# An encoder on one core: TensorE's products too in a computed order, the last down group in other pieces, the final norm's squares through banks

## The chip, the core and the metric

The kernel runs on one core of a Trainium2 chip. The metric is device time in microseconds (us), as the median of several executions. One execution is also recorded by the hardware profiler; the profile's own clock runs from the first to the last instruction of the program (the span). Engines are named as in the profile: PE is TensorE (matrix products; PEld are its weight loads, which overlap the products), DVE is VectorE, ACT is ScalarE, POOL is GpSimd, SP is SyncE, which here only issues transfers (DMAs). SBUF is the on-chip memory that all engines use; a bank is one of eight pieces of the memory into which TensorE writes its sums.

## The reference

Two layers of an encoder over 512 tokens of width 1024, everything in float32. Each layer adds three things to x, and a last norm ends it:

```python
for l in range(DEPTH):
    x = x + hybrid_mixer(rms_norm(x, norm_mix[l]), w_in[l], na_rpb[l], gqa_q_norm[l], gqa_k_norm[l], w_out[l], rows, cos, sin)
    x = x + memory_cross_attention(rms_norm(x, norm_mem_q[l]), rms_norm(mem, norm_mem_kv[l]), w_mem_q[l], w_mem_kv[l], w_mem_o[l])
    x = x + conv_ffn(rms_norm(x, norm_ffn[l]), w_up[l], conv_w[l], conv_b[l], w_down[l])
return rms_norm(x, norm_final)

def conv_ffn(h, w_up, conv_w, conv_b, w_down):
    u = h @ w_up                                   # 1024 -> 2 x 2816
    up = jnp.pad(u, ((0, 0), (1, 1), (0, 0)))
    u = up[:, :-2] * conv_w[0] + up[:, 1:-1] * conv_w[1] + up[:, 2:] * conv_w[2] + conv_b
    gate, val = jnp.split(u, 2, axis=-1)
    return (jax.nn.silu(gate) * val) @ w_down      # 2816 -> 1024

def rms_norm(x, g):
    return x * lax.rsqrt(jnp.mean(x * x, axis=-1, keepdims=True) + EPS) * g
```

The mixer holds neighbourhood attention (8 heads) and grouped-query attention (8 heads over 2 key heads, with normed and rotated queries and keys) on one projection of x; the memory attention has 4 heads over 256 memory tokens.

## The kernel before

**Data.** x is kept transposed: eight tiles xT[0..7], each 128 features x 512 tokens. A float32 product is made of three fast ones: each operand is split into a rounded part hi and a rest lo, and `mm3` (L730) adds hi x hi, hi x lo and lo x hi in one bank. So every weight piece is loaded ("raw", two buffers), cast on ACT into hi (L647) and subtracted on POOL into lo (L648); hi and lo have four buffers each (`N_W`), and `get_w` (L651) emits the splits of the next two pieces (`AHEAD`) when one is taken.

**Stages.** In each layer: projections woven with the two attentions (`weave`, with `Filler` handing out projection products between the attention's steps), the memory attention, then the feed-forward part, with its 22 chunks of the inner width in three groups, `GROUPS = [(0, 8), (8, 7), (15, 7)]`. A chunk's up products (two of 24 products of 512 columns) are followed by the convolution and the gate on DVE and ACT (`up_finish`, L1617), whose result acts[j] is again a hi and lo pair. After a group's chunks its down products add to xT.

**The last group.** `down_last` (L1666) does layer 2's third group, chunks 15 to 21, and the final norm with it, in two halves of 256 tokens. For each of the eight rows m it sums 7 x 3 products of 256 columns in a bank; DVE adds the bank to xT[m] (L1704); `Norm.square` (L833) squares the row on ACT (L835) into an SBUF tile and DVE adds it to the running sum of squares (L843, L846), the last square staying apart; DVE scales the row by the norm's gain (`scale`, L1674). In the first half the first four rows leave out the last chunk at first (`N_LATE`). Weight pieces are 7 x 128 columns of one row m, loaded once for both halves: the first two pieces are in the hi and lo buffers, six in tiles of the "r" pool ("Pr" in `plan_down`), so that they are still there in the second half. `Norm.stat` (L849) sums over the features with small products against a column of ones, first for the running sum, then for the last square, each followed by warm-up products in the second half, and POOL makes the power -1/2 (L867). `Norm.spread` (L869) spreads it over a bank with products against the identity (L798), and ACT copies the bank to SBUF (L801). `finish` multiplies: DVE takes the bank for six rows (L1684), POOL the copy for two (L1682); five DMAs write the half's output. The first half's statistics and finish stand after rows 1 and 3 of the second half.

**What sets the order.** The program is emitted as a list per engine. PE and SP keep the written order: `PE` is a `Counted(InOrder)`, whose `keep` marks each product. For ACT, DVE and POOL the class `Order` (L306) computes an order at the end of the program (L1729). It models every instruction's duration (`Step.times`), the buffers and the transfers; `due` (L393) gives each instruction a latest start, counted back from the products, which are taken to follow one another; `run` (L411) plays the program, and `choose` picks on each free engine the ready instruction with the earliest latest start. Where a product comes more than 150 ns late in the model, its due time is moved forward by that (`credit`) for the next of 16 rounds; the round with the earliest end is kept. An engine on the chip executes its list strictly in that order.

Of the kernel before, what the change touches and what calls it, by code (L numbers as in the profile page):

```python
# [1 line left out]

# [16 lines left out]
P = 128  # L19
# [12 lines left out]
GROUPS = [(0, 8), (8, 7), (15, 7)]  # L32
EPS = 1e-6
# [19 lines left out]
N_RAW, N_W, N_R, N_T, N_S, AHEAD, AHEAD_HELD, N_WARM, N_LATE, N_FIRST = 2, 4, 21, 14, 24, 2, 5, 7, 4, (8, 16)  # L53
# [18 lines left out]
class Counted(InOrder):  # L72
# [4 lines left out]
    def matmul(self, out, lhsT, rhs, **k):  # L77
        n = 1
        for d in rhs.shape[1:]:
            n *= d  # L80
        self.ns += max(107.0, (n + 32) / 2.4)
        return self.keep(self.engine.matmul(out, lhsT, rhs, **k))  # L82


class Free:


    def __init__(self, engine):
        self.engine = engine

    def __getattr__(self, name):
        return getattr(self.engine, name)
# [110 lines left out]
ROUNDS = 16  # L203
# [102 lines left out]
class Order:  # L306

    FREE = ("ACT", "DVE", "POOL")  # L310

    def __init__(self, tc, kept):
# [98 lines left out]
    def run(self):  # L411
# [3 lines left out]
        ready, free_at = [0.0] * n, dict.fromkeys(HAND_OVER, 0.0)  # L415
# [9 lines left out]
        order, late, product = {e: [] for e in self.FREE}, [], None  # L425
# [3 lines left out]
        def earliest(j):  # L429
# [18 lines left out]
            return max(t, free_at[steps[j].engine])  # L448

        def choose(e):  # L450

            known = [(t, j) for j in open_[e] for t in [earliest(j)] if t is not None]
# [39 lines left out]
        def over_(s, t, end):  # L492

            for q in self.after[s.index]:
                need[q] -= 1
                begun = s.engine == "PE" == steps[q].engine or (s.index, q) in self.loose
                ready[q] = max(ready[q], t if begun else end + self.wait(s, steps[q]))
                if not need[q] and steps[q].engine in self.FREE:
# [7 lines left out]
        while len(issued) < n or moving:  # L506
            best = None
            for e in HAND_OVER:
                if e in self.FREE:
                    c = choose(e)  # L510
                elif at[e] < len(written[e]):
# [16 lines left out]
            if e in self.FREE:  # L528
                open_[e].remove(j)
                order[e].append(s)  # L530
            else:
                at[e] += 1
# [12 lines left out]
            free_at[e] = t + s.busy  # L545
            issued.add(j)
            for name in s.names:
# [5 lines left out]
            if s.dma:  # L553
                if not moving:
                    clock = max(clock, t)
                moving.append([t + DMA_NS, s.bytes, j])
            else:
                over_(s, t, t + s.takes)
# [5 lines left out]
def encoder_kernel(ctx: ExitStack, tc: tile.TileContext, t: dict, out: bass.AP):  # L564
    nc = tc.nc
    kept = set()
    PE, SP = Counted(tc, nc.tensor, kept), InOrder(tc, nc.sync, kept)
# [65 lines left out]
    def emit_split(act=ACT, cuts=2):  # L633
# [6 lines left out]
        if eng[1:] == "r":  # L640
            hi, lo = rtile((nk, ncol)), rtile((nk, ncol))
        else:
            hi = wpool.tile([P, nk, ncol], F32R, tag="hi", name=nm("hi"))
            lo = wpool.tile([P, nk, ncol], F32R, tag="lo", name=nm("lo"))
# [6 lines left out]
    def get_w(key, ahead=AHEAD):  # L651
# [3 lines left out]
        while ahead < min(len(plan), n + 1 + AHEAD_HELD) and plan[ahead][4][1:] == "r":  # L655
            ahead += 1
# [137 lines left out]
    def row_rep(rstd, n, tag, bufs, copy):  # L794

        pr = ps_t()
        for b in range(n):
            PE.matmul(pr[:, b * P : (b + 1) * P], rstd[:, b : b + 1].to_broadcast([P, P]), ident,  # L798
                      start=True, stop=True)
# [1013 lines left out]
```

## Time and profile before

| | us |
|---|---|
| median of 3 executions | 1351.61 (1350.64 to 1352.07) |
| the profiled execution | 1351.96 |
| its span | 1350.1 |
| PE busy | 1337.5 |
| DVE busy | 902.1 |
| POOL busy | 698.8 |
| ACT busy | 681.0 |

The granted clock of TensorE is 0.999 of full speed over the span. In the rows below, `L82` is the line of the helper through which every product goes, so products are told apart by their tiles: `mm<-r,hi` is a sum in an "mm" bank from a tile of the "r" pool and one of the hi buffers. A row of the timeline gives start, duration, engine, line, operation, tiles and shape; consecutive instructions of a kind are merged (x84), and brackets hold the engine's idle time before it and what ended it. A row of the chain gives start, length and what it consists of. A row of the stretches gives the stretch, its length, and then each engine's busy time and number of instructions, the granted clock, the DMA share and GB/s. Products are pipelined: the shown time of one overlaps the next.

### The profile page before, as it was taken

What the parts mean: (1) busy time and instruction counts of PE and PEld (TensorE: products, weight loads), DVE (VectorE), ACT (ScalarE), POOL (GpSimd) and SP (SyncE); (2) the same over time, 40 slices, a digit from 0 to 9 for tenths busy, and PEclk for the clock granted to TensorE, in tenths of its full rate; (3) what the DMA queues carried; (4) which work ended last, traced back from release to release, by engine and by line L of the source; (5) the groups of instructions that cost most, each with busy time, mean ns of one, the idle gap of its engine ahead of it and who ended that gap; (6) DMA issues with size and microseconds to landing.
All of it is one profiled execution on the core that took longest, in us unless ns stands there. A gap on an engine that the chain in (4) does not pass through costs nothing.

```text
span 1350.1 us, 19133 instructions
## 1 busy us (share of the span) xinstructions
PE 1337.5 (99%) x7018; PEld 1146.4 (85%) x7018; DVE 902.1 (67%) x1598; ACT 681.0 (50%) x1258; POOL 698.8 (52%) x483
## 2 busy tenths in 40 slices
PE   9999999999999999999999999999999999999997
PEld 7898899888888888888898888988888888888887
DVE  6678874775984388178546678746769825862874
ACT  6776676564442244233557667855644423432441
POOL 2558766626444443443744576655554444444541
PEclk9999999999999999999999999999999999999999
DMA  7773222313333333332455531233233333333321
GB/s 217 201 190 109 79 63 73 116 45 96 96 103 98 94 94 94 109 94 82 127 155 164 140 106 49 79 95 94 63 94 98 104 94 94 93 95 109 90 83 63
DMA packets 219214, 139.88 MB, mean 104 GB/s; under 512 B 6000, under 2 KB 212080, under 8 KB 219120
## 3 DMA queue, kind: packets, MB, share of 16 engines
q1 hardware_dynamic: 218432, 138.13, 35.4%
q8 instruction: 56, 0.92, 0.3%
q10 hardware_dynamic: 688, 0.52, 0.1%
q14 instruction: 38, 0.31, 0.1%
HBM read 126.05 MB, written 2.10 MB: 95 GB/s over the span
## 4 chain that ended last, share of the span: by engine, by line
PE 93%; DVE 2%; DMA 1%; issue 1%; ACT 1%; POOL 1%; SPq 0%; DVEq 0%; POOLq 0%; ACTq 0%
PE mm L82 81%; PE sc L82 7%; PE tr L69 4%; PE tr L82 1%; DMA raw<-in_w_down 1%; POOL r L648 1%; DMA xT<-in_xT 0%; DVE t L846 0%; DMA raw<-in_w_in 0%; ACT r L1075 0%; SPq L69 0%; DVE r L875 0%; ACT hi L647 0%; ACT t L1257 0%; DVE r L1684 0%
## 5 line engine op out<-in xcount | busy, mean ns | idle before, releaser
L648 POOL TENSOR_TENSOR lo<-raw,hi 128x1024 fp32r<-128x1024 f32 (+2 forms) x268 | 511.5, 1919 | 498.6 <-ACT hi L647 494.7
L82 PE MATMUL mm<-xg,hi 128*128 128x512 f32 x1920 | 595.0, 391 | 0.0
L82 PEld LDWEIGHTS mm<-xg,hi 128*128 128x128 f32 x1920 | 356.1, 188 | 70.9
L647 ACT CAST hi<-raw 128x512 fp32r<-128x512 f32 (+2 forms) x276 | 226.3, 839 | 318.8 <-PE mm L82 267.8
L82 PE MATMUL mm<-xg,lo 128*128 128x512 f32 x960 | 373.9, 389 | 0.0
L82 PE MATMUL mm<-r,hi 128*128 128x512 f32 (+1 forms) x1096 | 316.3, 372 | 0.6 <-DVE r L1641 0.5
L1635 DVE SCALAR_TENSOR_TENSOR t<-t,par,t 128x7 f32<-128x7 f32 (+1 forms) x352 | 251.2, 773 | 25.0 <-ACT t L1628 25.0
L82 PEld LDWEIGHTS mm<-r,hi 128*128 128x128 f32 x1096 | 198.6, 189 | 35.6 <-DVE r L1641 0.7
L82 PEld LDWEIGHTS mm<-xg,lo 128*128 128x128 f32 x960 | 180.2, 188 | 37.9
L82 PE MATMUL mm<-r,lo 128*128 128x512 f32 (+1 forms) x548 | 203.6, 372 | 0.0
L82 PEld LDWEIGHTS mm<-r,lo 128*128 128x128 f32 x548 | 103.3, 188 | 17.9
L881 POOL TENSOR_SCALAR t<-t,s 128x512 f32<-128x512 f32 (+1 forms) x112 | 67.9, 622 | 75.0 <-DVE s L1323 36.1
L1620 DVE TENSOR_TENSOR t<-mm,rep 128x512 f32<-128x512 f32 x88 | 60.0, 686 | 63.0 <-PE mm L82 47.3
L1664 DVE TENSOR_TENSOR xT<-xT,mm 128x512 f32<-128x512 f32 x32 | 22.0, 686 | 104.5 <-PE mm L82 104.5
L1640 ACT CAST r<-t 128x512 fp32r<-128x512 f32 x44 | 27.3, 620 | 101.7 <-DVE t L1638 101.7
L1638 DVE TENSOR_TENSOR t<-t,t 128x512 f32<-128x512 f32 x44 | 68.2, 1551 | 4.3 <-ACT t L1637 0.5
L82 PE MATMUL sc<-r,r 128*128 128x256 f32 (+1 forms) x352 | 70.7, 333 | 0.3 <-DVE r L1081 0.3
L1628 ACT ACTIVATE t<-t,par 128x512 f32<-128x512 f32 x88 | 67.0, 806 | 1.2 <-DVE t L1620 1.2
L1317 ACT ACTIVATE t<-sc,s,qr 128x512 f32<-128x512 f32 x64 | 49.3, 775 | 32.2 <-DVE s L881 32.2
L82 PE MATMUL mm<-r,r 128*128 128x256 f32 (+1 forms) x428 | 62.5, 297 | 1.7 <-POOL r L648 1.1
L69 PE MATMUL tr<-ident,t 128*128 128x128 f32 x456 | 61.0, 273 | 0.7 <-DVE s L1267 0.7
L82 PEld LDWEIGHTS mm<-r,r 128*128 128x128 f32 x428 | 56.4, 191 | 5.0 <-POOL r L648 1.3
(160 smaller groups left out, 1607.8 us busy)
## 6 DMA issues: line engine op xcount, KB each, us to landing
raw<-in_w_up SPq DMA_DIRECT2D x88, 512.0 KB, 3.8
raw<-in_w_in SPq DMA_DIRECT2D x33, 512.0 KB, 4.1
raw<-in_w_down SPq DMA_DIRECT2D x32, 448.0 KB, 3.7
raw<-in_w_mem_kv SPq DMA_DIRECT2D x16, 512.0 KB, 3.8
raw<-in_w_down SPq DMA_DIRECT2D x16, 512.0 KB, 4.0
r<-in_bias SPq DMA_DIRECT2D x16, 384.0 KB, 4.9
r<-r SPq DMA_DIRECT2D x22, 256.0 KB, 5.6
raw<-in_w_out SPq DMA_DIRECT2D x8, 512.0 KB, 3.7
```

The lines of the kernel that those rows point to most:

```text
L69: return lambda *a, **k: self.keep(op(*a, **k))
L82: return self.keep(self.engine.matmul(out, lhsT, rhs, **k))
L647: act.copy(hi[:, k], raw[:, k])
L648: (POOL if eng[0] == "P" else DVE).tensor_sub(lo[:, k], raw[:, k], f(hi)[:, k])
L881: eng.tensor_scalar(e, e, sums[:, col : col + 1], 1.0, op0=ALU.mult, op1=ALU.mult)
L1317: ACT.activation(e, sc[j], AF.Exp, bias=nmx[:, c], scale=qrs[i][:, col : col + 1], accum_out=sums[:, c])
L1620: DVE.tensor_mul(u, us[side], ffn.rep)
L1628: ACT.activation(cc, u, AF.Identity, bias=par[:, l, CB + ch : CB + ch + 1], scale=w[1])
L1635: DVE.scalar_tensor_tensor(cc[:, dst], u[:, src], wi, cc[:, dst], op0=ALU.mult, op1=ALU.add)
L1638: DVE.tensor_mul(cs[0], cs[0], cs[1])
L1640: ACT.copy(acts[j][0], cs[0])
L1664: DVE.tensor_add(xT[m], xT[m], pm)
```

## The change

- **The order of the products.** `Counted` no longer keeps the written order. `Order` computes an order for PE too: `product_next` takes, of the next unissued products in the written list (at most 240 looked at), the first that can start within 60 ns of PE being free, else the one that can start earliest.
- **The planner's rounds.** Each round's order is played twice more with random extra durations (up to 4%) and transfer times, and the sum of those ends decides which round is kept. A product counts as late already when its operands come less than 100 ns (`MARGIN`) ahead of it; the due times are moved by random shares of the lateness, kept per stretch of 250 instructions. POOL's choice lets a due DVE instruction with two SBUF operands go first.
- **The last group.** Its seven chunks are cut in two parts, `LAST = [(15, 4), (19, 3)]`. The first part (four chunks) is summed for all 512 tokens and added to xT; the second (three chunks) in two halves of 256 tokens, with the norm as before. Pieces are 256 output features wide, two rows each, all in the hi and lo buffers.
- **The final norm.** The squares of rows 1 to 5 are written to "sc" banks. The square of row 6 isn't added to the running sum but goes into the first small products; one of the two warm-ups goes. The gain is applied by ACT, into the output tile. The spread is multiplied in place, two rows at a time: by POOL for the first half, and by DVE (six rows) and POOL (two) for the second, whose copy for POOL comes from a second bank. Four DMAs write a half's output.
- **In the first layer**, the key's rest is copied to the other 64 partitions by POOL, where DVE subtracted it a second time.

```diff
+LAST = [(15, 4), (19, 3)]
...
-class Counted(InOrder):
+class Counted(Free):
...
-        return self.keep(self.engine.matmul(out, lhsT, rhs, **k))
+        return self.engine.matmul(out, lhsT, rhs, **k)
...
-ROUNDS = 16
+ROUNDS, REPLAYS, MARGIN, SHARES, STRETCH, SEED = 16, 2, 100.0, (0.0, 0.0, 0.5, 1.0, 2.0), 250, 0
+DMA_SPREAD = 1900.0, 3100.0
+AHEAD_MOST, PATIENCE = 240, 60.0
...
+    ORDERED = FREE + ("PE",)
...
-        self.credit, best = {}, None
-        for _ in range(ROUNDS):
+        best, kept_credit, self.credit, draw = None, {}, {}, random.Random(SEED)
+        for n in range(ROUNDS):
             self.due()
-            end, order, late = self.run()
+            _, order, late = self.run()
+            end, lost = 0.0, {}
+            for i in range(REPLAYS):
+                e, _, more = self.run(order, random.Random(i))
+                end, late = end + e, late + more
             if best is None or end < best[0]:
                 best = end, order
-            for j, by in late:
-                self.credit[j] = self.credit.get(j, 0.0) + by
+            for j, by, _ in late:
+                lost[j // STRETCH] = lost.get(j // STRETCH, 0.0) + by
+            for w in range(len(self.steps) // STRETCH + 1):
+                mine = {j: c for j, c in self.credit.items() if j // STRETCH == w}
+                if w not in kept_credit or lost.get(w, 0.0) < kept_credit[w][0]:
+                    kept_credit[w] = lost.get(w, 0.0), mine, [x for x in late if x[0] // STRETCH == w]
+            self.credit = {}
+            for w, (_, mine, then) in kept_credit.items():
+                self.credit.update(mine)
+                for j, _, by in then:
+                    self.credit[j] = self.credit.get(j, 0.0) + by * draw.choice(SHARES) / (1 + REPLAYS)
...
-            return max(t, free_at[steps[j].engine])
+            return t
+        def earliest(j):
+            t = possible(j, ready)
+            return t if t is None else max(t, free_at[steps[j].engine])
...
+            if e == "POOL":
+                for q in open_["DVE"]:
+                    if steps[q].two_from_sbuf() and self.latest[q] < self.latest[j]:
+                        t = earliest(q)
+                        if t is not None and soon < t + 1 < soon + busy and soon + busy > self.latest[q]:
+                            t += steps[q].busy
+                            if t <= self.latest[j]:
+                                return max(t, soon), j
...
+        def product_next():
+            mine, i, seen, best = written["PE"], at["PE"], 0, None
+            while i < len(mine) and seen < AHEAD_MOST:
+                j = mine[i]
+                i += 1
+                if j in issued:
+                    continue
+                seen += 1
+                t = earliest(j)
+                if t is not None and (best is None or t < best[0] - PATIENCE):
+                    best = t, j
+                if best is not None and best[0] <= free_at["PE"] + PATIENCE:
+                    break
+            return best
...
-                if product is not None and t > product + 150:
-                    late.append((j, t - product))
+                short = MARGIN - (t - possible(j, fed))
+                if product is not None and short > 0:
+                    late.append((j, t - product, t - product + short))
...
+        if (l, g) == (DEPTH - 1, len(GROUPS) - 1):
+            for i, rows in enumerate(LAST):
+                for mp in range(4):
+                    cols(("down", "ab"[i], mp), t["w_down"][l], *rows, 256 * mp, 256)
+            return
         for m in range(KC):
-            held = l + 1 == DEPTH and g + 1 == len(GROUPS) and m >= 2
-            cols(("down", g, m), t["w_down"][l], *GROUPS[g], P * m, P, "Pr" if held else "P")
+            cols(("down", g, m), t["w_down"][l], *GROUPS[g], P * m, P)
...
+    def row_bank(rstd, n):
         pr = ps_t()
         for b in range(n):
             PE.matmul(pr[:, b * P : (b + 1) * P], rstd[:, b : b + 1].to_broadcast([P, P]), ident,
                       start=True, stop=True)
+        return pr
...
-            sq = tmp((self.n,))
+            sq = tmp((self.n,)) if self.gcol is not None or c == 0 or c >= KC - 2 else ps_s()[:, : self.n]
             e = act.activation(sq, xT[c][:, self.cols], AF.Square)
             eng = eng or (POOL if self.gcol is not None and c < KC - 1 else DVE)
             if self.acc is None:
                 self.acc = sq
-            elif c == KC - 1 and self.gcol is None:
-                self.last = sq
+            elif c >= KC - 2 and self.gcol is None:
+                self.last.append(sq)
...
-            def sums(sq):
+            def sums(*sqs):
                 pv = ps_t()
                 for b in range(nb):
-                    PE.matmul(pv[:, b : b + 1], sq[:, b * P : b * P + P], ones, start=True, stop=True)
+                    for i, sq in enumerate(sqs):
+                        PE.matmul(pv[:, b : b + 1], sq[:, b * P : b * P + P], ones, start=i == 0, stop=i == len(sqs) - 1)
                 return pv[:, 0:nb]
 
-            if self.last is None:
+            if not self.last:
                 self.rstd, self.var = rsqrt(sums(self.acc), nb, 1.0 / D, factor)
                 return
 
             part, v, self.rstd = small(nb), small(nb), small(nb)
-            DVE.tensor_scalar(part, sums(self.acc), 1.0 / D, EPS, op0=ALU.mult, op1=ALU.add)
-            warm()
-            DVE.scalar_tensor_tensor(v, sums(self.last), 1.0 / D, part, op0=ALU.mult, op1=ALU.add)
+            DVE.tensor_scalar(part, sums(self.acc, self.last[0]), 1.0 / D, EPS, op0=ALU.mult, op1=ALU.add)
+            DVE.scalar_tensor_tensor(v, sums(self.last[1]), 1.0 / D, part, op0=ALU.mult, op1=ALU.add)
...
-                    DVE.tensor_sub(k[o, 1], pm[r], f(k[r, 0]))
+                    POOL.tensor_copy(k[o, 1], k[r, 1])
...
-        def down_last(g):
...
+        def down_last():
+            parts = [[acts.pop(j) for j in range(j0, j0 + nj)] for j0, nj in LAST]
+            ws = {}
+            def product(pm, i, m, ops):
+                if (i, m // 2) not in ws:
+                    ws[i, m // 2] = get_w(("down", "ab"[i], m // 2))
+                gemm_T(pm, ws[i, m // 2], ops, range(len(ops)), 0, len(ops) - 1, slice(P * (m % 2), P * (m % 2) + P))
+            for m in range(KC):
+                pm = ps_mm()
+                product(pm, 0, m, parts[0])
+                DVE.tensor_add(xT[m], xT[m], pm)
+            def finish(norm, y, last=False):
+                pr = row_bank(norm.rstd, NB // 2)
+                rep = tmp((256,))
+                ACT.copy(rep, (row_bank(norm.rstd, NB // 2) if last else pr)[:, :256])
+                for k in (0, 2, 6, 4):
+                    eng, by = (DVE, pr) if last and k < 6 else (POOL, rep)
+                    v = y[k // 4][:, k % 4 : k % 4 + 2]
+                    eng.tensor_mul(v, v, by[:, :256].unsqueeze(1).to_broadcast([P, 2, 256]))
+                for i, k in enumerate((0, 2, 4, 6)):
                     (ACT_IN_ORDER if last and i % 2 else SP).dma_start(
+                        out[k * P : (k + 2) * P, norm.cols].rearrange("(k p) n -> p k n", p=P), y[k // 4][:, k % 4 : k % 4 + 2])
+            norms, ys = [], []
             for half in range(2):
                 cs = slice(256 * half, 256 * half + 256)
+                hops = [(hi[:, cs], lo[:, cs]) for hi, lo in parts[1]]
                 norms.append(Norm(cols=cs))
+                ys.append([rtile((4, 256), F32) for _ in range(2)])
                 for m in range(KC):
+                    pm = ps_mm()[:, :256]
+                    product(pm, 1, m, hops)
+                    DVE.tensor_add(xT[m][:, cs], xT[m][:, cs], pm)
+                    norms[half].square(m)
+                    ACT.activation(ys[half][m // 4][:, m % 4], xT[m][:, cs], AF.Copy, scale=gfin[:, m : m + 1])
                     if half == 1 and m == 1:
                         norms[0].stat()
                     elif half == 1 and m == 3:
+                        finish(norms[0], ys[0])
             norms[1].stat(warm=lambda: warm_up(3))
+            finish(norms[1], ys[1], True)
```

More of the change, by code (lines that the diff above doesn't have):

```diff
@@ L424, in run, with possible @@
         issued, landed, shared = set(), set(), {"DVE": 0.0, "POOL": 0.0}
-        order, late, product = {e: [] for e in self.FREE}, [], None
+        order, late, product = {e: [] for e in self.ORDERED}, [], None
         moving, clock, last = [], 0.0, 0.0
-        def earliest(j):
+        def possible(j, ready):
             if need[j] or self.kept.get(j, -1) >= 0 and self.kept[j] not in issued:
@@ L497, in over_ @@
                 ready[q] = max(ready[q], t if begun else end + self.wait(s, steps[q]))
+                if s.engine != "PE":
+                    fed[q] = max(fed[q], end + self.wait(s, steps[q]))
                 if not need[q] and steps[q].engine in self.FREE:
@@ L544, in run @@
                 shared["DVE"] = t + s.busy
-            free_at[e] = t + s.busy
+            slow = 1.0 if draw is None or e not in self.FREE else 1.0 + 0.04 * draw.random()
+            free_at[e] = t + s.busy * slow
             issued.add(j)
+            while e == "PE" and at[e] < len(written[e]) and written[e][at[e]] in issued:
+                at[e] += 1
             for name in s.names:
@@ L977, in encoder_kernel @@
         if u == len(ready):
[L978 to L981 removed]
+            ready.append(tuple(wpool.tile([P, KC, P], F32R, tag=tag, name=nm(tag)) for tag in ("hi", "lo")))
         raw, (hi, lo) = raws[u], ready[u]
@@ L1693, in down_last @@
                 norms.append(Norm(cols=cs))
-                rows = []
+                ys.append([rtile((4, 256), F32) for _ in range(2)])
                 for m in range(KC):
-                    if half == 0:
-                        ws.append(get_w(("down", g, m)))
-                    rows.append(ps_mm()[:, :256])
-                    late = half == 0 and m < N_LATE
-                    gemm_T(rows[m], ws[m], hops, range(nj - 1 if late else nj), 0, nj - 1)
-                    for i in [m] if not late else range(N_LATE) if m == N_LATE - 1 else []:
-                        if late:
-                            gemm_T(rows[i], ws[i], hops, [nj - 1], 0, nj - 1)
-                        DVE.tensor_add(xT[i][:, cs], xT[i][:, cs], rows[i])
-                        norms[half].square(i)
-                        scale(half, i)
+                    pm = ps_mm()[:, :256]
[3 more added lines that the diff above has]
+                    ACT.activation(ys[half][m // 4][:, m % 4], xT[m][:, cs], AF.Copy, scale=gfin[:, m : m + 1])
```

79 lines of the change are left out of this document (30 added, 49 removed).

## The prediction, on record before the result was known

> **What bounds the kernel.** Read first: the head of the page, the busy time by stretches, and what TensorE waited for.
>
> ```profile
> span 1350.1 us, 19133 instructions
> PE 1337.5 (99%) x7018; PEld 1146.4 (85%) x7018; DVE 902.1 (67%) x1598; ACT 681.0 (50%) x1258; POOL 698.8 (52%) x483
> ...
> core 0: us, PE busy (x) PEld busy (x) DVE busy (x) ACT busy (x) POOL busy (x), PEclk, DMA share, GB/s
> 300.00:670.00 370.00, 370.00 (x1642) 306.70 (x1641) 239.78 (x323) 146.33 (x192) 183.19 (x86) 1.00 0.33 97
> 965.00:1285.00 320.00, 320.00 (x1421) 265.22 (x1420) 211.00 (x276) 121.72 (x155) 155.12 (x67) 1.00 0.34 97
> ...
> engine line waited for: us in total, times, longest us
> PE tr L82 <- POOL ident masks.py:199: 1.3, 1, 1.3
> PE mm L82 <- POOL r L648: 1.1, 1, 1.1
> PE mm L82 <- DVE r L1096: 0.7, 1, 0.7
> PE tr L69 <- DVE s L1267: 0.7, 1, 0.7
> PE mm L82 <- ACT t L1257: 0.5, 1, 0.5
> PE mm L82 <- DVE r L1641: 0.5, 1, 0.5
> PE sc L82 <- DVE r L1081: 0.3, 1, 0.3
> PE tr L82 <- POOL s L867: 0.3, 1, 0.3
> PE tr L82 <- DVE t L846: 0.2, 1, 0.2
> PE sc L82 <- ACT xg L69: 0.2, 1, 0.2
> ```
>
> TensorE bounds it: idle for 12.6 of 1350.1 us. Its ten waits make 5.8 of these; the rest is the end, after its last product (at 1343.45, by a row below). In the two long feed-forward stretches it is busy to the last hundredth, so nothing is to be won there and an altered order can only lose. What a better order can reach is the waits elsewhere; what the new last group can reach is two of the ten (POOL r L648, DVE r L1641), some columns, and the end.
>
> How long one product holds TensorE is read from the chain, as pitch and not as duration:
>
> ```profile
> 328.00 342.76 PE mm L82 x1512
> 1330.01 10.07 PE mm L82 x84
> ```
>
> 342.76 us over 1512 products of 512 columns is 0.2267 us each; 10.07 over 84 products of 256 columns is 0.120. A product's shown time overlaps the next one's, so a wait costs more than its idle time. These rows give by how much:
>
> ```profile
> L82 PE MATMUL mm<-xg,hi 128*128 128x512 f32 x1920 | 595.0, 391 | 0.0
> 1305.79 0.28 PE L82 MATMUL mm<-r,lo 128*128 128x256 f32 x1
> 1316.06 2.54 PE L82 MATMUL mm<-r,r 128*128 128x256 f32 x19 [1.11 <-POOL r L648]
> 287.33 1.95 PE L82 MATMUL mm<-r,r 128*128 128x512 f32 x6
> 774.94 0.63 PE L69 MATMUL tr<-ident,t 128*128 128x128 f32 x4 [0.66 <-DVE s L1267]
> 775.32 0.71 PE L82 MATMUL mm<-xg,hi 128*128 128x512 f32 x2
> ```
>
> A product of 512 columns is shown with 0.39 us (the first row is a group of the page, its mean in ns) and one of 256 with 0.28. Against the pitch that is 0.16 more, so each wait costs 0.16 us above its idle time. The row at 287.33 shows a loss with no idle time at all: six products should end 5 x 0.2267 + 0.39 = 1.52 us after they begin, and take 1.95.
>
> **The change, part by part.**
>
> *Columns of the last group.* Before, 8 rows x 7 x 3 x two halves are 336 products of 256 columns: 336 x 0.120 = 40.3 us. After, 8 x 4 x 3 = 96 of 512 columns (21.8 us) and 8 x 3 x 3 x 2 = 144 of 256 (17.3): 39.0. **-1.3 us**, all on the path. The trace puts the fixed part of a product near 13 ns. [...]
>
> *The two waits of the last group.* The wait at 1316.06 stands behind this supply:
>
> ```profile
> 1312.90 0.94 ACT L647 CAST r<-raw 128x896 fp32r<-128x896 f32 x1 [2.32 <-DMA raw<-in_w_down]
> 1313.92 2.09 POOL L648 TENSOR_TENSOR r<-raw,r 128x896 fp32r<-128x896 f32 x1 [1.86 <-ACT r L647]
> 1314.19 2.09 DVE L846 TENSOR_TENSOR t<-t,t 128x256 f32<-128x256 f32 x1 [1.25 <-ACT t L835]
> 1308.49 0.41 DVE L846 TENSOR_TENSOR t<-t,t 128x256 f32<-128x256 f32 x1
> 1316.65 0.42 ACT L835 ACTIVATE t<-xT 128x256 f32<-128x256 f32 x1 [2.49 <-DVE xT L1704]
> ```
>
> A piece of weights is loaded, cast on ACT, subtracted on POOL: 3.0 us after it lands, and in the first half one row eats a piece in 21 x 0.12 = 2.5 us. After, an "a" piece (1024 columns of work, like those of the up products) feeds 24 products, 5.4 us, the pace at which the 965 to 1285 stretch never waits; and rows 15 to 18 are done long before, so the wait for the last activation (L1641) goes under 21.8 us of "a" products. The four "b" pieces fit the four buffers; the fourth gets its buffer when the "a" part ends, needs some 2.6 us (0.94 and 2.09 scaled by 768/896) and is wanted after 6 x 9 x 0.12 = 6.5. Cover gone, it costs 2 us at most. Both waits go: 0.5 + 1.1 + 2 x 0.16 = **-1.9**, at worst 0.
>
> *Squares through banks; scaling on ACT.* Row L846 takes 0.41 us alone and 2.09 under POOL's subtraction, with both operands in SBUF. One operand in a bank should keep it at 0.41. TensorE waited for none of these, so this counts as 0, but it is what allows the faster rows: in the "b" halves a row lasts 9 x 0.12 = 1.08 us, and needs on DVE two operations of 0.41 and on ACT a square (0.42 at L835, last row) and a scaling, taken as the same. Both fit with 0.24 to spare; a backlog of one row at the end would cost 1.1.
>
> *Sums.* The sixth square goes unadded into the statistic, as its own products:
>
> ```profile
> 1323.48 0.95 PE L82 MATMUL tr<-ones,t 128*128 128x1 f32 x8
> ```
>
> Four more records at about 0.11 in the middle: **+0.4**. At the end they lie beside the last square. One of two warm-ups goes, from the shadow of the same square: 0.
>
> *The end.* From the last product on:
>
> ```profile
> 1342.74 0.71 PE L82 MATMUL tr<-ident,s 128*128 128x128 f32 x4 [0.25 <-POOL s L867]
> 1343.56 0.37 ACT L801 COPY rep<-tr 128x256 f32<-128x256 f32 x1 [2.51 <-PE tr L82]
> 1343.97 2.08 DVE L1684 TENSOR_TENSOR r<-xT,tr 128x256 f32<-128x256 f32 x6 [2.06 <-ACT rep L801]
> 1344.01 1.41 POOL L1682 TENSOR_TENSOR r<-xT,rep 128x256 f32<-128x256 f32 x2 [1.33 <-ACT rep L801]
> 780.53 1.27 POOL L1278 TENSOR_TENSOR t<-t,t 128x512 f32<-128x512 f32 x1
> 1344.75 1.75 SPq L69 DMA_DIRECT2D out<-r  x3
> 1293.68 0.69 DVE L1641 TENSOR_TENSOR r<-t,r 128x512 fp32r<-128x512 f32 x1 [0.69 <-ACT r L1640]
> ```
>
> DVE now waits for ACT's copy of the bank, 0.4 us; with a bank of its own it need not. Its three 512-wide products cost about what six 256-wide ones do (3 x 0.69, by the last row, against 2.08). POOL's bank comes 4 x 0.11 = 0.4 later, and one 512-wide product (1.27 at L1278) replaces two (1.41): it ends at about 1345.7, against 1345.4. Four output DMAs on two queues in place of five. **-0.4**; between -0.7 (the first transfer begins earlier and the rest follows) and +0.6 (the last, now twice as large, waits for POOL). The first half's four products go to POOL, 5.1 us inside the second half's 8.6; their DMAs queue on SP, behind which no weights are left.
>
> *The near copies.* In the first layer two DVE subtractions become POOL copies:
>
> ```profile
> 36.20 0.69 DVE L1081 TENSOR_TENSOR r<-sc,r 64x512 fp32r<-64x512 f32 x1
> 36.57 3.78 POOL L648 TENSOR_TENSOR lo<-raw,hi 128x512 fp32r<-128x512 f32 x3 [7.32 <-ACT hi L647]
> 770.49 0.61 POOL L1274 COPY t<-s 128x512 f32<-128x512 f32 x1
> ```
>
> DVE gains 1.4 us; a copy (0.61) may queue behind a weight subtraction (1.26). What waits is the first score product (0.3 idle). Taken **0**, between -0.5 and +1.3.
>
> *The computed order.* Outside start, last group and end the waits are L1096, L1267, L1257, L1081 and L846: 2.4 us idle, 3.2 with 0.16 each; losses without idle time like that at 287.33 (0.4) bring it, as my estimate, to some 4.6. At 774.94 transposes wait while the next product in the list (775.32, mm<-xg,hi) had its operands; letting it pass is what the new planner does. It can't help where nothing else is ready, and its clock is a model. Bounds: all go (-4.6), or as much arises anew (+4.6). I take half, **-2.3**, because at least the largest (L1267, L1257) lie amid projection products that wait for nothing.
>
> **Sum.** -1.3 - 1.9 + 0.4 + 0 - 0.4 + 0 - 2.3 = -5.5: a span of 1344.6. The profiled execution took 1351.96, 1.86 more than its span, and stands 0.35 over the median of 1351.61: 1344.6 + 1.86 - 0.35 = **1346.1**. All bounds at their best give -8.6, 1343.0; at their worst +5.6, 1357.2.
>
> **Rivals.**
> - *All the waits outside the last group go too*: 4.6 instead of 2.3, 1343.8. For it: they are few and single. Against: at 36.22 and 287.33 the stage is short of other work. 22 in 100.
> - *The order wins nothing*, because the planner keeps the written order or trades wait for wait: only -3.2, 1348.4. The two stretches without waits speak for it. 12 in 100.
> - *The last group is fed late*: "b" pieces queue behind squares and scalings on ACT (8 x 0.84 of 8.6 us is taken), so a wait of 2 us comes back and a backlog of 1.1 meets the end; with no gain elsewhere 1351.5, no change. 11 in 100.
> - *Slower: TensorE pulls products ahead of their operands.* It runs its list strictly in order, so where the model has an operand too early, TensorE stands although the written list's next product was ready. A miss costs what the waits above do, 0.5 to 0.7 and 0.16 more, about 0.75. With the last group's 3.2 kept, 8 net misses (5.9 / 0.75) make it 0.2% slower; 12 give 1357.4. For it: every engine's order changes in the attention stages, where POOL and DVE block each other (the L846 rows). Against: now only ten waits arise under the same kind of model. 10 in 100.
>
> The forecast itself, 1344 to 1348, has 45 in 100. A change within 0.2% (2.7 us) is about what a measurement of this kernel can't tell from none; below 1348.9 counts as faster. So faster 0.79 (45 + 22 + 12), same 0.11, slower 0.10. The range reaches from a little below the best bounds, 1342.0, to 1352.0, which takes in the fed-late case; the forecast's own is 1344 to 1348.
>
> **What would show it.** Right: no wait for POOL r or DVE r in the last 50 us; 96 + 144 products there; the adds of squares at 0.41 throughout; DVE's last products beginning before ACT's copy ends; fewer than eight waits in the list. Wrong: new waits of TensorE on DVE, ACT or POOL between 30 and 300 or 670 and 965, less than full busy time in the feed-forward stretches, or the end longer than 10 us after the last product.

## The result and the profile after

The changed kernel takes 1347.28 us (median of 8 executions, 1346.94 to 1348.21) where the kernel before, on the same chip, takes 1351.28 (8 executions): a ratio of 0.9971, with a 95% interval of 0.996 to 0.9982. It is 4.0 us faster, or 0.29%. The forecast was 1346.1, with 1348 as the upper end of its own range.

Head of the page, stretches, and the list of what TensorE waited for, of the kernel after:

```profile
span 1345.5 us, 18965 instructions
PE 1336.2 (99%) x6928; PEld 1142.0 (85%) x6928; DVE 895.1 (67%) x1577; ACT 688.9 (51%) x1274; POOL 703.5 (52%) x486
...
300.00:670.00 370.00, 370.00 (x1642) 306.59 (x1640) 239.28 (x322) 146.24 (x192) 183.77 (x86) 1.00 0.33 97
965.00:1285.00 320.00, 320.00 (x1422) 265.18 (x1420) 208.02 (x276) 121.73 (x154) 154.05 (x67) 1.00 0.33 98
1285.00:1316.00 31.00, 31.00 (x138) 25.70 (x137) 21.59 (x30) 9.92 (x14) 13.27 (x6) 1.00 0.24 76
...
engine line waited for: us in total, times, longest us
PE tr L95 <- POOL ident masks.py:199: 1.3, 1, 1.3
PE mm L95 <- DVE r L1149: 0.8, 1, 0.8
PE tr L95 <- DVE r L948: 0.3, 1, 0.3
PE tr L95 <- POOL s L940: 0.3, 1, 0.3
PE tr L95 <- DVE t L919: 0.2, 1, 0.2
PE sc L95 <- ACT xg L72: 0.2, 1, 0.2
PE tr L95 <- ACT t L1327: 0.2, 1, 0.2
```

Seven waits and 3.3 us of idle time in place of ten and 5.8. No wait for POOL r or DVE r is left in the last group, and TensorE is busy from 1285 to 1316 without a gap. But the largest wait of all that the order could reach, DVE r L1149 at 741 us, is new at that size (L1079 in the kernel before is the same line, and TensorE lost 0.2 us to it there).

The first and last products of the last group, and the end, of the kernel before and of the one after (a row of five merged products has a pitch of 0.12, so its last begins at 1339.80):

```profile
1296.14 0.40 PE L82 MATMUL mm<-r,hi 128*128 128x256 f32 x2
1339.32 0.76 PE L82 MATMUL mm<-r,r 128*128 128x256 f32 x5
```

```profile
1294.97 0.39 PE L95 MATMUL mm<-r,hi 128*128 128x512 f32 x1
1335.65 0.28 PE L95 MATMUL mm<-r,lo 128*128 128x256 f32 x1
...
1338.52 1.16 PE L95 MATMUL tr<-ident,s 128*128 128x128 f32 x8 [0.25 <-POOL s L940]
1339.27 1.88 DVE L1759 TENSOR_TENSOR r<-r,tr 128x512 f32<-128x512 f32 x3 [1.58 <-PE tr L95]
1339.72 0.37 ACT L1755 COPY t<-tr 128x256 f32<-128x256 f32 x1 [2.48 <-PE tr L95]
1340.17 1.27 POOL L1759 TENSOR_TENSOR r<-r,t 128x512 f32<-128x512 f32 x1 [1.70 <-ACT t L1755]
```

The group, from its first product to its last, falls from 43.66 to 40.68 us; what follows, up to the end of the span, from 1350.1 - 1339.8 = 10.3 to 1345.5 - 1335.65 = 9.9. DVE's last products now begin 0.75 us after the spread, before ACT's copy, where it was 1.23. All that lies ahead of the group falls by 1.2 us (1296.14 to 1294.97) in these two profiles.

### The profile page after: what moved, and what is told of

Same layout as the page of the kernel before. It is cut to its first block, busy times and chain, and to the rows that moved or that the text cites. A ratio compares the mean times of both kernels' runs of the same rounds, so it can differ in the third digit from the quotient of the medians.

```text
span 1345.5 us, 18965 instructions
## 1 busy us (share of the span) xinstructions
PE 1336.2 (99%) x6928; PEld 1142.0 (85%) x6928; DVE 895.1 (67%) x1577; ACT 688.9 (51%) x1274; POOL 703.5 (52%) x486
## 4 chain that ended last, share of the span: by engine, by line
PE 93%; DVE 3%; ACT 2%; DMA 1%; issue 1%; POOL 0%; SPq 0%; POOLq 0%; DVEq 0%; ACTq 0%
PE mm L95 82%; PE sc L95 6%; PE tr L1408 2%; PE tr L95 1%; PE tr L1250 1%; PE tr L1603 1%; ACT t L1228 0%; DMA r<-in_w_in 0%; DVE t L919 0%; DVE r L1166 0%; ACT r L1164 0%; DVE r L948 0%; DVE r L1149 0%; DMA raw<-in_w_in 0%; DVE sc L1222 0%
## 5 line engine op out<-in xcount | busy, mean ns | idle before, releaser
L714 POOL TENSOR_TENSOR lo<-raw,hi 128x1024 fp32r<-128x1024 f32 (+3 forms) x274 | 525.3, 1927 | 521.3 <-ACT hi L713 521.1
L713 ACT CAST hi<-raw 128x512 fp32r<-128x512 f32 (+3 forms) x282 | 232.7, 841 | 338.1 <-PE mm L95 284.5
L95 PE MATMUL mm<-r,hi 128*128 128x512 f32 (+1 forms) x1200 | 343.8, 370 | 0.0
L95 PEld LDWEIGHTS mm<-r,hi 128*128 128x128 f32 x1200 | 216.5, 189 | 36.5
L95 PE MATMUL mm<-r,lo 128*128 128x512 f32 (+1 forms) x600 | 221.7, 369 | 0.0
L95 PEld LDWEIGHTS mm<-r,lo 128*128 128x128 f32 x600 | 113.1, 188 | 19.1
L1708 DVE TENSOR_TENSOR t<-t,t 128x512 f32<-128x512 f32 x44 | 74.3, 1689 | 4.9 <-ACT t L1707 0.9
L95 PEld LDWEIGHTS sc<-r,r 128*128 128x128 f32 x352 | 51.9, 190 | 5.8 <-ACT t L1387 1.5
L95 PE MATMUL mm<-hi,xg 128*128 128x256 f32 x256 | 49.3, 284 | 0.8 <-DVE r L1149 0.8
L1711 DVE TENSOR_TENSOR r<-t,r 128x512 fp32r<-128x512 f32 x44 | 34.5, 785 | 19.3 <-ACT r L1710 19.3
```

Of the source, the lines that this page charges most:

```text
L95: return self.engine.matmul(out, lhsT, rhs, **k)
L713: act.copy(hi[:, k], raw[:, k])
L714: (POOL if eng[0] == "P" else DVE).tensor_sub(lo[:, k], raw[:, k], f(hi)[:, k])
L1708: DVE.tensor_mul(cs[0], cs[0], cs[1])
L1711: DVE.tensor_sub(acts[j][1], cs[0], f(acts[j][0]))
```

## The experiments

Each difference is the kernel's median against that of the kernel before measured beside it. "Group" and "end" are read from the trace as above.

| kernel | median us | against before | group | end |
|---|---|---|---|---|
| after | 1347.28 | -4.00 | 40.68 | 9.88 |
| e1 last group alone | 1348.49 | -2.57 | 40.68 | 9.88 |
| e2 order alone | 1351.48 | +0.42 | 42.56 | 10.31 |
| e3 after, products in written order | 1351.15 | +0.09 | 40.68 | 9.90 |
| e4 after, random number 1 | 1349.17 | -1.89 | 40.68 | 9.89 |
| e5 after, old rounds | 1349.63 | -1.63 | 40.68 | 9.90 |
| e6 after, squares in SBUF | 1348.99 | -2.27 | 40.68 | 10.16 |
| e7 after, cut 3 + 4 | 1349.08 | -2.18 | 41.00 | 9.91 |
| e8 after, random number 2 | 1349.37 | -1.89 | 40.68 | 9.88 |
| e9 near keys alone | 1353.75 | +2.86 | 43.36 | 10.29 |
| e10 last group and near keys | 1351.19 | +0.30 | 40.68 | 9.89 |
| e11 after, a square late | 1350.69 | -0.20 | 40.68 | 9.89 |
| e12 after, 128 rounds | 1346.90 | -3.99 | 40.68 | 9.89 |

**The parts alone (e1, e2).** e1 takes from the diff the hunks of the last group and the final norm, e2 those of `Counted`, `Order` and its constants.

> The kernel before with the new last group alone: TensorE in the written order, the old rounds of the planner, the near keys still subtracted on DVE. My theory (the parts add up; the last group and the end are worth 3.4 us: 3.1 from the group's first product to its last, 0.35 behind it): 1347.5 to 1348.3, and the list of TensorE's waits keeps L1096, L1267, L1257 (0.5 to 0.8 each) and loses the two of the last group. Rival (the last group only runs without waits because products may pass one another): a wait or two of 0.5 us or more stays in the last 50 us, and the time is 1349 to 1350.5.

> The kernel before with the computed order of the products and the new rounds of the planner alone; last group, final norm and near keys as before. My theory: 1.2 us is all that the order gives outside the last group, and the last group's two waits (1.9 us) stay in part, since the weights come no earlier: 1348.5 to 1350.5. Rival 1 (the order is worth as much as the group, also in the old last group, where products of other rows can go first): below 1348. Rival 2 (the order is worth nothing or costs): 1351 or more.

What TensorE waited for in e1:

```profile
PE mm L84 <- DVE r L1099: 0.7, 1, 0.7
PE tr L71 <- DVE s L1270: 0.7, 1, 0.7
PE mm L84 <- DVE r L884: 0.6, 1, 0.6
PE mm L84 <- ACT t L1260: 0.5, 1, 0.5
PE sc L84 <- DVE r L1084: 0.3, 1, 0.3
```

The group and the end are as in the changed kernel to 0.01 us, without any product passing another: the rival falls, and the time is 0.2 us above my range. The three old waits stay, and one is new (DVE r L884, at 84 us); its 0.75 us of lost pitch is about what lies between the 3.4 us that group and end give and the 2.57 measured. e2 gives nothing (its 0.42 us are within the noise): its old last group is 1.1 us shorter, and new waits ahead of it take that back (0.8 for DVE t L913 at 259 us is the largest). The expected 1348.5 to 1350.5 was too low; rival 2 held.

**What the order is worth in the changed kernel (e3, e5).** In e3 the products keep the written order again:

```diff
-class Counted(Free):
+class Counted(InOrder):
...
-        return self.engine.matmul(out, lhsT, rhs, **k)
+        return self.keep(self.engine.matmul(out, lhsT, rhs, **k))
```

e5 keeps the products' order and has the rounds of the kernel before (its loop over `self.run()`, and a product late from 150 ns on).

> The changed kernel with TensorE held to the written order, while the planner keeps its new rounds for ACT, DVE and POOL. My theory: the free order of the products is worth about what the sum of waits fell by outside the last group, 1 to 1.5 us: 1348 to 1349. Rival 1 (the new rounds, not TensorE's order, removed those waits): 1347.0 to 1347.6, the same as the changed kernel. Rival 2 (the order also carries the last group): 1349.5 or more, with a wait of over 0.5 us in the last 50 us.

> The changed kernel with TensorE's computed order kept, but the planner's rounds as before: one play per round, a product late where it comes over 150 ns after the one before it, due times moved by the full lateness, the round with the earliest end kept. Theory A (what counts is that products may pass one another; the plan is luck within 2 us): 1347.5 to 1349.5. Theory B (the new rounds, with plays of random durations and the margin of 100 ns, make the gain over the last group alone, which took 1348.49): 1348.5 or more, with waits of over 0.5 us at three or more places between 30 and 300 or 670 and 965 us.

e3 loses the whole 4 us, though its last group has no wait. Its list shows where:

```profile
PE sc L95 <- DMA r<-r: 1.2, 1, 1.2
PE tr L95 <- ACT t L1327: 0.6, 1, 0.6
PE mm L95 <- ACT t L1327: 0.5, 1, 0.5
PE mm L95 <- DVE r L1149: 0.4, 1, 0.4
PE sc L95 <- ACT hi L713: 0.4, 1, 0.4
```

So neither my 1 to 1.5 us nor rival 2's place (the last group) was right: most of the loss is in the first layer's attention (the waits at 76, 77 and 102 us). e5 meets theory B's number and its waits, but e4 and e8 below have the new rounds and stand within 0.3 us of it, so the new rounds aren't what makes the difference either.

**The plan as luck (e4, e8, e12).** Only the planner's start or length is changed:

```diff
-ROUNDS, REPLAYS, MARGIN, SHARES, STRETCH, SEED = 16, 2, 100.0, (0.0, 0.0, 0.5, 1.0, 2.0), 250, 0
+ROUNDS, REPLAYS, MARGIN, SHARES, STRETCH, SEED = 16, 2, 100.0, (0.0, 0.0, 0.5, 1.0, 2.0), 250, 1
```

(2 in e8; 128 rounds and number 0 in e12.)

> The changed kernel with the planner's random numbers started at 1 instead of 0: the same program, another plan. My theory: the waits outside the last group (0.94 at 741 us, 0.44 at 119.6, 0.36 at 142) are misses of the planner's model in one plan among many, so they move to other places and their sum changes by up to 1.5 us: 1346 to 1349, with the last group and the end within 0.3 us of the changed kernel. Rival (the waits are forced by the program): the same waits at the same places, within 0.3 us of the changed kernel's time.

> The changed kernel with the planner's random numbers started at 2. By the planner's own play this plan ends 1.7 us later than that of the changed kernel (number 1: 1.2 later, and measured 1.9 slower). My theory: the planner's end is a guide to the chip, within about 1 us: 1348.2 to 1350. Rival (the plans differ on the chip by chance alone): as likely below 1347.3 as above 1349.2.

> The changed kernel with 128 rounds of the planner instead of 16, number 0 as before: a longer search. By the planner's own play the plan found ends 0.44 us earlier than that of the changed kernel. Theory (the planner's end is a guide within about 0.5 us, with numbers 1 and 2 measured 1.9 and 2.1 us slower where it said 1.2 and 1.7): 1346.2 to 1347.4, the fastest of all. Rival (what is left on the chip is not in the model): 1347.5 to 1349.5.

With the other two numbers 2.1 us of the 4.0 are gone, ahead of the last group alone. Some waits do stay in place (DVE r L1149 costs 0.92 to 0.94 us of pitch in e4, e5, e6, e8 and the changed kernel, 0.54 in e7 and e12), so my theory of wandering misses held in part, and e4 lies just above its range; what e4, e5, e6, e7 and e8 have and the changed kernel hasn't is a wait of about 1 us ahead of the small products of the norm at 259 to 262 us (DVE t L919) or of the key norms at 100 to 112 (ACT t, the square). Against the changed kernel's plan, the planner's own end was 1.2, 1.7 and -0.4 us off for e4, e8 and e12; measured, each against its kernel before, 2.1, 2.1 and 0.0. It tells the two slower plans from the others, but not to half a microsecond. e12 is no faster than the changed kernel: its median is 0.4 us lower, and so is that of the kernel before beside it (1350.89).

**The near keys (e9, e10).** e9 is the kernel before with this edit, e10 has the last group's hunks too:

```diff
-                    DVE.tensor_sub(k[o, 1], pm[r], f(k[r, 0]))
+                    POOL.tensor_copy(k[o, 1], k[r, 1])
```

> The kernel before with the near keys alone: two POOL copies in place of two DVE subtractions in the first layer. In every kernel so far that has them, the waits at 36 and 38 us were 0.16 and 0.24 us long in pitch, and in every one without them 0.74 to 0.86 and 0.34 to 0.47. My theory (this edit, which I had put at nothing, is worth 0.9 us by itself): the same two waits shrink here, and the time is 0.4 to 1.4 us under that of the kernel before. Rival (the new order shortens them): they stay, and the time is within 0.3 us.

> The kernel before with the new last group and the near keys, and neither the computed order of the products nor the new rounds. Theory (the order gave nothing net outside the last group; group and end 3.4, near 0.9, less what waits this plan has by chance): 3.2 to 4.4 us under the kernel before, as the changed kernel, which is 4.0 under it. Rival (the order of the products is a part of the gain): 3 us or less, 1 us or more behind the changed kernel.

The two early waits shrink as I said (to 0.16 and 0.24 us of pitch), and the kernel is 2.9 us slower. The gain is lost at once, 40 us later. TensorE's waits there in e9:

```profile
75.81 0.47 PE L82 MATMUL sc<-r,r 128*128 128x256 f32 x2 [0.56 <-DMA r<-r]
76.97 0.95 PE L82 MATMUL sc<-r,r 128*128 128x256 f32 x6 [0.69 <-DMA r<-r]
...
PE tr L82 <- ACT t L1257: 1.2, 1, 1.2
```

What SP's queue waited for ahead of two copies of keys (r<-r), and their issue, first in the kernel before and then in e9; the last row is the issue of the same two in the changed kernel:

```profile
SPq L69 <- DVE lo L648: 4.0, 1, 4.0
64.24 1.10 SPq L69 DMA_DIRECT2D r<-r  x2
...
SPq L69 <- DVE lo L648: 7.9, 1, 7.9
67.50 1.11 SPq L69 DMA_DIRECT2D r<-r  x2
...
67.90 1.11 SPq L72 DMA_DIRECT2D r<-r  x2
```

With the edit the planner orders this whole stretch anew. A weight load at the head of SP's queue waits for DVE's subtraction of an earlier weight, which ends at 65.9 instead of 62.5, and the copies queued behind it are issued at 67.5 instead of 64.2. They land some 8 us later, and the score products (sc) wait for them. The changed kernel issues them later still, and TensorE doesn't wait: from 75.03 to 76.47 it has twelve projection products (mm) ahead of the score products, where in e9 they come behind them. In e10 the same waits stand at 75 to 77 and 101 us, and in e3, which also has the edit and the written order, at 76, 77 and 102. So it is the written order together with this edit that fails, and the computed order that passes other products ahead there.

Both of my theories fell, and e10's rival held. The edit's price is not local: it is 2.9 us in the old kernel and 2.9 beside the new group (e10 against e1). The computed order with its rounds is worth 4.3 us once the edit is in (e10 against after, each against its kernel before), but 2.2 with the plans of e4 and e8.

**Squares, and the cut (e6, e7).**

```diff
-            sq = tmp((self.n,)) if self.gcol is not None or c == 0 or c >= KC - 2 else ps_s()[:, : self.n]
+            sq = tmp((self.n,))
```

```diff
-LAST = [(15, 4), (19, 3)]
+LAST = [(15, 3), (18, 4)]
```

> The changed kernel with the squares of the final norm's rows 1 to 5 in SBUF tiles instead of banks. The plan of everything before changes too, so the last 50 us are read by themselves. My theory: DVE's adds of squares (0.42 us now) have two SBUF operands and stretch to 0.8 to 1.7 us where POOL subtracts or multiplies (four products of 1.26 us in the second half), so that DVE falls behind and either the group (40.7 us from its first product to its last) or the end grows by 0.3 to 2 us. Rival (DVE has the time anyway): the adds stretch but group and end stay within 0.2 us.

> The changed kernel with the last group cut 3 + 4 instead of 4 + 3: a row of the second part takes 1.44 us on TensorE instead of 1.08, in which DVE has 0.84 to do and ACT 0.91. My theory: TensorE's columns alone set the group's length, so it is 0.3 us longer (72 x 0.2267 + 192 x 0.120 = 39.4 against 39.0) and the end the same. Rival (DVE or ACT can't keep up with 1.08 us a row, and a backlog meets the end): the end is 0.3 us or more shorter than in the changed kernel.

The adds of squares (least, median and most of eight, in ns) with squares in banks, and then in SBUF with the products of POOL and the start of the spread:

```profile
L919 DVE TENSOR_TENSOR t<-t,sc x8: 414/422/422, 1321.6 to 1335.2; 128x256 f32<-128x256 f32 x8
...
1332.11 5.05 POOL L1759 TENSOR_TENSOR r<-r,t 128x512 f32<-128x512 f32 x4 [2.21 <-ACT t L1755]
```

```profile
L919 DVE TENSOR_TENSOR t<-t,t x8: 416/425/581, 1325.7 to 1339.3; 128x256 f32<-128x256 f32 x8
...
1336.78 5.38 POOL L1759 TENSOR_TENSOR r<-r,t 128x512 f32<-128x512 f32 x4 [2.81 <-ACT t L1755]
1342.87 1.16 PE L95 MATMUL tr<-ident,s 128*128 128x128 f32 x8 [0.46 <-POOL s L940]
```

The adds hardly stretch (0.58 at most, not 0.8 to 1.7): POOL pays instead, 5.38 us for four products in place of 5.05. They end at about 1342.1, right where the last power starts (1342.12); it starts 0.29 us after the statistic that it takes, in the changed kernel 0.08, and the spread waits 0.46 instead of 0.25. The group stays at 40.68 and the end grows by 0.28: banks are worth 0.3 us here, a little under my range. Where these adds, with both operands in SBUF, meet POOL's products, the loser is mostly POOL (the adds' median goes from 422 to 425 ns).

e7 settles the columns: 41.00 against 40.68 us is +0.32, as worked out from the pitches (39.4 against 39.0 us of products), and the end is the same to 0.03. TensorE's columns set the group's length; the 1.6 us above 39.0 are 16 small products, the first half's sums and spread.

**A wait beside tiny products (e11).** The plan is left as it is; two repetitions of one square, with the same values, are hidden from the planner:

```diff
             ACT.activation(sq, pm, AF.Square)
+            for _ in range(2 if (l, g) == (0, 0) else 0):
+                unplanned.add(ACT.activation(sq, pm, AF.Square).ins.name)
```

> The changed kernel with the very same plan, but ACT squares one bank of the first layer (line 1327, the square that TensorE waits for at 142 us) three times over, with the same values; the planner does not see the two repetitions, 1.2 us. TensorE waits 0.8 to 1.2 us longer there, right ahead of eight tiny products (128x2). [...] Rival (a wait costs its length): every execution within 1.3 us of the others, as in the changed kernel, at 1348.1 to 1348.6.

I took it that behind such a wait the clock drops to half in some executions, and that the median is 1 to 2.5 us over the changed kernel. What made me suspect it is e8: stretches around its wait at 100 us (columns as before; the granted clock is the third figure from the end), and TensorE's rows there:

```profile
99.00:101.00 2.00, 1.06 (x8) 0.64 (x6) 1.97 (x6) 1.46 (x4) 1.14 (x1) 1.00 0.45 110
101.00:103.00 2.00, 2.00 (x15) 2.00 (x15) 1.93 (x9) 0.00 (x0) 0.00 (x0) 0.77 0.41 91
103.00:105.50 2.50, 2.50 (x7) 1.92 (x7) 0.00 (x0) 2.08 (x8) 1.38 (x2) 0.51 0.75 215
105.50:108.00 2.50, 2.50 (x17) 2.13 (x16) 1.19 (x4) 2.48 (x7) 2.50 (x3) 1.00 0.00 0
...
100.51 1.05 PE L95 MATMUL tr<-pairs,t 128*128 128x2 f32 x8 [0.94 <-ACT t L1327]
101.43 1.56 PE L95 MATMUL mm<-r,r 128*128 128x256 f32 x8
102.78 1.05 PE L95 MATMUL mm<-xg,hi 128*128 128x512 f32 x2
```

A wait of 0.94 us and eight products of two columns, and then the granted clock is 0.5 for some 3.4 us (0.23 x 2.0 and 0.49 x 2.5 us lost in the second and third row, over 0.5): products of 512 columns come every 0.427 us (102.78 + 0.427 = 103.21, then 103.64). Its profiled execution is one of three out of ten that took over 1351 us. e4 and e7 show the same behind their wait at 259 us (clock 0.50 from 260.8 to 264.0 and from 261.4 to 264.3).

In e11 the wait comes, at another place than I had read (the first such square feeds the products at 110.8 us, not at 142), and twice as long as I meant:

```profile
110.78 1.05 PE L95 MATMUL tr<-pairs,t 128*128 128x2 f32 x8 [2.13 <-ACT t L1330]
```

Its executions, with the mean granted clock of each:

```
1348.50 0.998   1348.55 0.998   1349.13 0.999
1350.44 0.997   1350.59 0.997   1350.79 0.996   1350.80 0.996
1351.88 0.995   1351.93 0.995   1353.47 0.996
```

The three with the full clock are 1.2 to 1.9 us over the changed kernel; the seven with less are 3.2 to 6.2 over it, with the same program. The changed kernel's eight lie within 1.3 us, and its slowest (1348.21) has the lowest clock too, 0.997. The rival, that a wait costs its length, falls. The median, 3.4 us over, is also above my theory's 1 to 2.5. The profiled execution was one of the undisturbed, so its trace doesn't show the half clock behind the wait: the clock is 1.00 from 107 to 117 us. By the means, as an estimate, the executions at 0.995 lack 0.003 of 1347 us against those at 0.998, which is some 8 us at half clock, two or three stretches like e8's; where they lie no trace shows. Over all kernels: the changed kernel, e1 and e12, which in their profiles have no wait of 0.4 us or more ahead of a run of eight tiny products, spread by 1.0 to 1.3 us, and the kernel before, which has none either (its 1.11 us at 1316 stand among full products), by 1.3 to 2.3 beside one kernel or another, but for one execution of 97 at 1354.31; those with one by 2.6 to 6.4. Not all of that spread is the clock: e6's profiled execution took 1351.68 at a clock of 0.999. Its trace has waits at 77, 100, 112 and 262 us that cost 0.43, 0.85, 1.18 and 1.15 us of pitch; whether its faster executions (1348.3 to 1349.2) have them too stays open.

## Why the prediction was right or wrong

*Columns, waits and sums of the last group* (-1.3, -1.9, +0.4, together -2.8): measured -2.98, and the same to 0.01 us in every kernel with the new group and the 4 + 3 cut. The pitches of 0.2267 and 0.120 carried it; e7 confirms them with the opposite sign, and with them the fixed part of about 13 ns (2 x 0.120 - 0.2267). The "b" pieces came in time.

*The end* (-0.4): -0.43, by the mechanism given: DVE no longer waits for ACT's copy. POOL's product now ends last, 2.9 us after the spread begins, where DVE's ended 3.3 after it.

*Squares and scaling at 0*: right for the group; 0.3 us at the end without them (e6), by POOL being late for the power and not by DVE's backlog, which I had named. The scaling on ACT, taken at 0.42 us, took 0.49 (L1775), which still fits a row.

*The near copies at 0, between -0.5 and +1.3*: wrong in kind. The two early waits fell (0.86 to 0.16, and 0.47 to 0.23 us of pitch, -0.9), but under the written order the edit costs 2.9 us. I looked at what waits for the instruction that is moved, and not at what the planner does with all others once one is moved.

*The computed order at -2.3* is the step that failed in size: what lies outside group and end, order and near copies together, is -4.0 + 3.4 = -0.6. Of the places I named, L1267, L1257 and the losses at 287 are gone, L1096 and L1081 are short and L846 stays; but new ones stand at 120, 142 and 741 us (0.44, 0.36 and 0.94 us of pitch). With that the rival "the order wins nothing", at 1348.4, was as near as the forecast. And it is the size in one plan: two other starts of the same search give 2.1 us less. The bounds, all waits gone or as many new ones, were the right kind of range; the middle was a guess.

*The rivals.* The group was never fed late. "Products ahead of their operands": e2, e4, e5, e6, e7 and e8 have new waits of 0.76 to 1.01 us, 0.9 to 1.2 with the 0.16, more than the 0.75 I had allowed a miss, and in e4, e7 and e8 the half clock came on top. Whether another product was ready at those moments isn't shown.

*What should show it*: no such wait in the last 50 us, adds at 0.42, DVE's products ahead of the copy's end and seven waits all came. One sign of being wrong came as well, the new waits between 30 and 300 and between 670 and 965 us. The sum agrees with the measured time to 1.2 us because group and end, 3.4 of the 4.0 us, were sized from measured rows, not because the order did what I thought; that the plan that was kept loses no more than it wins is luck.

## What to carry to other kernels

Price a change to a stage from the stage's own pitch, not from durations or from a saved wait: that part held to 0.2 us. Where a planner or a search orders the program, run it again from other starting points before you say what an edit is worth: here the plan alone moves the time by 2 us, and an edit that I had priced at nothing moved it by 2.9. Where one engine bounds the kernel, keep waits away from places where it has only tiny work: behind three such waits of 0.92 to 1.0 us, in e4, e7 and e8, TensorE's clock was half for some 3.4 us.

## What the runs showed of the hardware

In three profiles TensorE's clock fell to half behind a wait next to eight tiny products: behind 0.94 us in e8, 0.92 in e4 and 1.0 in e7. The clock of the stretches gives its length, as an estimate: (0.23 x 2.0 + 0.49 x 2.5) / 0.5 = 3.4 us in e8, (0.06 x 2.0 + 0.50 x 3.2) / 0.5 = 3.4 in e4, (0.12 x 1.7 + 0.50 x 2.9 + 0.02 x 2.7) / 0.5 = 3.4 in e7. Counted back from the end of the slow stretch, it began 1.6 us after the end of the wait in e8 (102.1 against 100.51) and 1.8 in e4 (260.6 against 258.76). The tiny products between took some 0.9 us (100.51 to 101.43 in e8).

It doesn't follow each time: behind e11's wait of 2.13 us the clock is 1.00 from 110.8 to 117 us. The profiled executions of e6, with waits of 1.01 and 0.99 us at 112 and 262 us, and of e9, with one of 1.23 at 102, have a mean clock of 0.999, the same as that of the changed kernel's. What decides it these runs don't show. Behind the waits of 0.66 to 1.11 us among full products or transposes in the kernel before (36, 775 and 1316 us) the clock is 1.00 in the stretches 36.5 to 44, 775.6 to 780 and 1317.5 to 1322; no run put such a wait there on purpose.

A DVE add of 512 columns with both operands in SBUF (L919) took 2.87 us beside POOL's weight subtraction, where the median of eleven is 0.69; in the kernel after this stands right ahead of the sums at 258 us, and TensorE still had other products:

```profile
254.21 5.17 POOL L714 TENSOR_TENSOR lo<-raw,hi 128x1024 fp32r<-128x1024 f32 x2
254.28 2.87 DVE L919 TENSOR_TENSOR t<-t,t 128x512 f32<-128x512 f32 x1 [0.68 <-POOL t L919]
```
